# Group B's chunk outputs read in three steps on three engines

## The chip, the cores and the metric

The kernel runs on one core of one Trainium2 chip. The metric is the time of one execution on the device in microseconds (us); what is given is the median of several executions. The engines of the core each work through a queue of their own in order, and wait for each other by semaphores: TensorE (PE in the rows, with its weight loads as PEld), VectorE (DVE), ScalarE (ACT), GpSimd (POOL) and SyncE (SP), which issues most of the transfers.

## What is computed

One layer of a network over 2048 latent and 256 context tokens of width 1024: a modulated norm, one wide input projection, two groups of eight heads, and an output projection. Group B is the one that matters here: a gated delta rule in both directions, in chunks. Cut to its step, with `s` the 128 x 128 state of a head and a direction:

```
v_new = u0_i - einsum(w_i, s)
s_new = d_last * s + einsum(k_dec, v_new)
o     = einsum(q_dec, s) + einsum(p_i, v_new)
out   = o_forward + flip(o_backward)
```

The output `o` of a chunk is a sum of two products. One needs only the old state, the other needs the chunk's solved values `v_new`. The next chunk needs `s_new` alone.

## The kernel before

Tokens are taken in groups of 256 (two chunks of 128). A step of the program takes one token group of one head through the input projection and, in the same step, other heads' later stages: group A's unit, the keys, values and inverse of group B, and group B's chunks, forward for one head and backward for another. All of that is written as generators that are interleaved, and a scheduler with a clock of its own then orders the instructions of every engine. So a change of a few lines moves instructions all over the program.

Group B's chunk is `chain` (L873). It runs 272 times (16 context chunks without an output among them), so 256 chunks have an output: 128 of them come first in their token group and leave `o` in the tile `op` (`first` is true), and 128 come second, load what the first left (`o<-od`, L971) and add to it in the tile `o`. For every chunk there is one PSUM tile `pc`, a bank with four 128 x 128 places, one buffer for each direction:

- L889 writes `p1`, the keys times the state, and L891 writes `o1`, the queries times the state
- L893 (VectorE) makes `r` of `p1`; L894 multiplies it by the masked inverse `zb` into `p2`
- L897 and L900 (ScalarE) read `p2` twice, as `ud` for the state and as `u` for the output
- L902 writes `p3` from `ud`; L907 (VectorE) makes the new state `S` of it
- L911 writes the second part of the output into `p1`, from the masked scores `P` and `u`
- `out` (L973) reads both parts: for `first`, L975 (ScalarE) copies the second part to `op`, and L976 (VectorE) scales `o1` by the column `neb` and subtracts the copy. Otherwise L978 (VectorE) adds the scaled `o1` to `o`, and L979 (VectorE) subtracts the second part

The tile `pc` is guarded as a whole: an instruction that writes one of its places waits until those written ahead of it have read the others. In the built order 233 of the 256 instructions of L911 wait for the state update L907, which reads another place, and L902 waits for `u` in 236 of 272. The next chunk of the direction gets the same buffer, so its L889 waits for L976 or L979.

GpSimd masks `zb` and `P` (L920), multiplies in the SiLU (L769), scales keys of group A (L1219), and adds a bias to rows of decays (L788). All that it works on here lies in SBUF.

Of the kernel before, what the change touches and what calls it, by code (L numbers as in the profile page):

```python
# [13 lines left out]
ALU = mybir.AluOpType  # L14
# [4 lines left out]
P = 128  # L19
# [601 lines left out]
class BHead:  # L621
# [251 lines left out]
    def chain(self, d, gi, c, out, last):  # L873


        K, nc, h = self.K, self.K.nc, self.h
        q = self.q[gi]
        s = self.S[d]
        i = gi * GC + c

        def col(t):
            return t[:, d, h, i:i + 1]
        zb = q[f"zb{d}"][:, c, :]
        pc = K.pc.tile([P, 4, P], F32, tag=f"c{d}", name="pc")
        p1, p2, p3, o1 = (pc[:, j, :] for j in range(4))
        if s is None:
            r = q["v"][:, c, :]
        else:
            nc.tensor.matmul(p1, lhsT=q["kT"][:, c, :], rhs=s, start=True, stop=True)  # L889
            if out is not None:  # L890
                nc.tensor.matmul(o1, lhsT=q["qT"][:, c * P:c * P + P], rhs=s, start=True, stop=True)  # L891
            r = K.ck.tile([P, P], F32, tag=f"r{d}", name="r")
            nc.vector.scalar_tensor_tensor(r, p1, col(K.neb), q["v"][:, c, :], op0=ALU.mult, op1=ALU.add)  # L893
        nc.tensor.matmul(p2, lhsT=zb, rhs=r, start=True, stop=True)  # L894
        if not last:
            ud = K.ck.tile([P, P], F32, tag=f"ud{d}", name="ud")
            nc.scalar.activation(ud, p2, AF.Copy, scale=q["rk"][:, 1 + d, c:c + 1])  # L897
        if out is not None:
            u = K.ck.tile([P, P], F32, tag=f"u{d}", name="u")
            nc.scalar.activation(u, p2, AF.Copy, scale=q["rk"][:, 0, c:c + 1])  # L900
        if not last:
            nc.tensor.matmul(p3, lhsT=q["kn"][:, c, :], rhs=ud, start=True, stop=True)  # L902
            sn = K.ck.tile([P, P], F32, tag=f"S{d}", name="S", bufs=2 + d)
            if s is None:
                nc.vector.tensor_copy(sn, p3)
            else:
                nc.vector.scalar_tensor_tensor(sn, s, col(K.el), p3, op0=ALU.mult, op1=ALU.add)  # L907
            self.S[d] = sn
        if out is not None:

            nc.tensor.matmul(p1, lhsT=q[f"P{d}"][:, c, :], rhs=u, start=True, stop=True)  # L911
            out(c, o1, col(K.neb), p1)

    def masked(self, gi, d):

# [36 lines left out]
    def group(self, gi, d, first):  # L952


        K, nc = self.K, self.K.nc
        q = self.q[gi]
        if not first and d == 1:
            self.load_kk(gi, "kb", BB)
            q["vq"] = K.rt.tile([P, 3, GT], F32, tag="vqb", name="vq", bufs=BB)
            nc.sync.dma_start(q["vq"], q.pop("vq_d"))  # L960
            self.vqp(gi)
            q["ZZ"] = K.rt.tile([P, GC, P], F32, tag="ZZb", name="ZZ", bufs=BB)
            nc.sync.dma_start(q["ZZ"], q.pop("ZZ_d"))
        self.masked(gi, d)
        if first:
            o = K.gt.tile([P, GC, P], F32, tag="op", name="op")
        else:
            g = K.ho.tile([P, GC, P], F32, tag="gl", name="gl")
            nc.sync.dma_start(g, q["gate"])
            o = K.ho.tile([P, GC, P], F32, tag="ol", name="o")  # L970
            nc.sync.dma_start(o, q["o"])  # L971

        def out(c, o1, neb, o2):  # L973
            if first:
                nc.scalar.copy(o[:, c, :], o2)  # L975
                nc.vector.scalar_tensor_tensor(o[:, c, :], o1, neb, o[:, c, :], op0=ALU.mult, op1=ALU.subtract)  # L976
            else:
                nc.vector.scalar_tensor_tensor(o[:, c, :], o1, neb, o[:, c, :], op0=ALU.mult, op1=ALU.add)  # L978
                nc.vector.tensor_tensor(o[:, c, :], o[:, c, :], o2, op=ALU.subtract)  # L979
        for j in range(GC):  # L980
            c = GC - 1 - j if d else j
            self.chain(d, gi, c, out, j == GC - 1 and gi == (1 if d else NG))
            if j < GC - 1:
                yield
        if first:
            od = q["o"] = K.drg.tile([P, GC, P], F32, tag="od", name="od")
            nc.sync.dma_start(od, o)
        else:
            head_out(K, o, g, q["rq"], gi, 1024 + P * self.h)
        yield  # L990
# [152 lines left out]
def head_out(K, o, g, rq, gi, col):  # L1143


    nc = K.nc
    n = o.shape[1]
    ss = K.sm.tile([P, n], F32, tag="oss", name="oss")
    jk = K.gt.tile([P, P], F32, tag="jk", name="jk")
    for c in range(n):  # L1150
        nc.scalar.activation(jk, o[:, c, :], AF.Square, accum_out=ss[:, c:c + 1])
    r = K.sm.tile([P, n], F32, tag="or", name="or")
    if rq is None:
        nc.gpsimd.tensor_scalar(ss, ss, 1.0 / (P * P), EPS, op0=ALU.mult, op1=ALU.add)
        pow_rsqrt(K, r, ss)
        nc.gpsimd.tensor_scalar(r, r, P ** -0.5, None, op0=ALU.mult)
    else:
        nc.gpsimd.tensor_mul(ss, ss, rq[:, 1, :])
        nc.gpsimd.tensor_scalar(ss, ss, EPS, None, op0=ALU.add)
        pow_rsqrt(K, r, ss)  # L1160
        nc.gpsimd.tensor_mul(r, r, rq[:, 0, :])
    for c in range(n):
        nc.vector.scalar_tensor_tensor(o[:, c, :], o[:, c, :], r[:, c:c + 1], g[:, c, :], op0=ALU.mult, op1=ALU.mult)
    t0 = (gi - 1) * n * P
    nc.scalar.dma_start(K.y_d[t0:t0 + n * P, col:col + P].rearrange("(c p) n -> p c n", p=P), o)
# [522 lines left out]
```

## Time and profile before

| | us |
|---|---|
| median of 3 runs | 3420.04 |
| lowest and highest | 3418.63, 3421.8 |
| the profiled execution | 3429.3 |
| its span, first to last instruction | 3427.6 |
| busy: PE, DVE, ACT, POOL | 3135.9, 2459.6, 1839.5, 1473.7 |

The profile is of one execution. An engine's busy time beside the span tells how near it is to being the bound; what ended its idle time tells whom it waited for. TensorE's busy time is modelled for pipelined matmuls, so it is not work at full speed. The granted clock is the share of TensorE's full clock that it was given.

### The profile page before, as it was taken

How to read it: one execution, taken by the hardware profiler on the slowest of the kernel's cores; microseconds unless marked ns; L12 is line 12 of the kernel's file. 1: busy time of each engine (PE TensorE's matmuls, PEld its weight loads, DVE VectorE, ACT ScalarE, POOL GpSimd, SP SyncE). 2: the span in 40 equal slices, each digit the busy share in tenths (PEclk: the TensorE clock that was granted, in tenths of full speed). 3: DMA queues.
4: the chain of work that ended last, by engine and by line, in shares of the span. 5: the costliest groups of instructions: out<-in, count | busy, mean ns of one | idle time of the engine just before them, and what ended most of it. 6: DMA issues, size and time to landing. Idle time of an engine off the chain costs nothing.

```text
span 3427.6 us, 95270 instructions
## 1 busy us (share of the span) xinstructions
PE 3135.9 (91%) x37768; PEld 2428.1 (71%) x37768; DVE 2459.6 (72%) x6531; ACT 1839.5 (54%) x4921; POOL 1473.7 (43%) x2534
## 2 busy tenths in 40 slices
PE   7878998999998999899999999999999899898998
PEld 3666777877787777777777777777777677755554
DVE  5867687778877876788678867886788677845332
ACT  5764555555655564556565555556455654644332
POOL 3525644465446443644464446444444243521010
PEclk9999999999999999999999999999999999999999
DMA  7744444454445444555455444544354544544331
GB/s 248 233 146 140 133 128 145 138 173 145 148 143 166 149 141 124 164 152 153 130 168 151 149 136 154 155 126 143 126 155 137 188 149 139 158 148 149 136 117 51
DMA packets 433475, 508.45 MB, mean 148 GB/s; under 512 B 110724, under 2 KB 336644, under 8 KB 420996
## 3 DMA queue, kind: packets, MB, share of 16 engines
q1 hardware_dynamic: 395908, 477.18, 44.4%
q10 hardware_dynamic: 37120, 25.18, 2.3%
q8 instruction: 297, 4.87, 0.6%
q14 instruction: 150, 1.23, 0.1%
HBM read 346.35 MB, written 155.88 MB: 147 GB/s over the span
## 4 chain that ended last, share of the span: by engine, by line
PE 39%; DVE 21%; DMA 16%; POOL 9%; ACT 8%; issue 5%; SPq 1%; ACTq 0%; DVEq 0%; POOLq 0%
PE po L1535 8%; DVE acc L690 5%; PE pm L405 4%; PE pm L407 4%; PE pm L406 4%; DMA raw<-in_w_in_dram 3%; DMA df<-dd 3%; DVE QK L1279 2%; POOL br L788 2%; POOL or L56 2%; DMA dc<-dc_d 2%; PE pz L398 2%; PE pz L396 2%; PE pz L397 1%; DMA y_d<-df 1%
## 5 line engine op out<-in xcount | busy, mean ns | idle before, releaser
L405 PE MATMUL pm<-h,whi 128*128 128x256 f16 x3256 | 900.3, 276 | 13.8 <-ACT pad L652 5.6
L407 PE MATMUL pm<-h,wlo 128*128 128x256 f16 x3256 | 898.9, 276 | 2.6 <-DVE wlo L388 2.6
L406 PE MATMUL pm<-h,whi 128*128 128x256 f16 x3256 | 899.3, 276 | 0.0
L690 DVE SCALAR_TENSOR_TENSOR acc<-pad,cw,acc 128x504 f32<-128x504 f32 (+1 forms) x768 | 585.6, 766 | 26.8 <-ACT acc L684 17.4
L396 PE MATMUL pz<-whi,h 128*128 128x384 f16 (+1 forms) x1152 | 362.0, 318 | 19.8 <-ACT pad L652 6.3
L406 PEld LDWEIGHTS <-whi 128*128 128x128 f16 x3328 | 330.9, 99 | 56.4 <-issue 14.4
L407 PEld LDWEIGHTS <-wlo 128*128 128x128 f16 x3328 | 330.7, 99 | 46.4 <-DVE wlo L388 3.9
L405 PEld LDWEIGHTS <-whi 128*128 128x128 f16 x3328 | 331.2, 100 | 44.9 <-ACT whi L385 2.0
L398 PE MATMUL pz<-whi,h 128*128 128x384 f16 (+1 forms) x1152 | 361.8, 318 | 0.0
L397 PE MATMUL pz<-wlo,h 128*128 128x384 f16 (+1 forms) x1152 | 361.4, 318 | 0.0
L1267 ACT COPY sk<-QK 128x512 f32<-128x512 f32 x384 | 242.4, 631 | 203.0 <-DVE QK L1279 150.6
L1279 DVE TENSOR_TENSOR QK<-QK,T 128x512 f32<-128x512 f32 x384 | 267.8, 697 | 49.0 <-ACT sk L1267 39.1
L1219 POOL TENSOR_SCALAR QK<-QK,omlb 128x256 f32<-128x256 f32 x144 | 154.9, 1083 | 210.4 <-ACT QK L1215 209.3
L788 POOL TENSOR_SCALAR br<-br,nbc 128x128 f32<-128x128 f32 x252 | 175.4, 712 | 81.5 <-DMA br<-row_d 55.3
L897 ACT ACTIVATE ud<-pc,rk 128x128 f32<-128x128 f32 x272 | 99.7, 367 | 171.8 <-PE pc L894 146.4
L920 POOL TENSOR_SCALAR_AFFINE_SELECT zb<-zb 128x256 f32<-128x256 f32 x144 | 68.4, 476 | 271.3 <-ACT zb L925 258.6
L1535 PEld LDWEIGHTS <-yh 128*128 128x128 f16 x1024 | 100.3, 98 | 110.2 <-ACT yh L1523 1.5
L542 POOL TENSOR_TENSOR g<-w,lm 128x128 f32<-128x128 f32 (+2 forms) x120 | 81.3, 677 | 208.6 <-DVE w L591 91.8
L397 PEld LDWEIGHTS <-h 128*128 128x128 f16 x1152 | 114.8, 100 | 78.6 <-issue 25.6
L398 PEld LDWEIGHTS <-h 128*128 128x128 f16 x1152 | 114.5, 99 | 61.5 <-issue 3.2
L396 PEld LDWEIGHTS <-h 128*128 128x128 f16 x1152 | 114.7, 100 | 56.7 <-issue 3.0
L920 POOL TENSOR_SCALAR_AFFINE_SELECT P<-vq 128x256 f32<-128x256 f32 x128 | 70.0, 548 | 181.1 <-PE pc L911 126.4
(368 smaller groups left out, 8074.9 us busy)
## 6 DMA issues: line engine op xcount, KB each, us to landing
h<-hT SPq DMA_DIRECT2D x72, 1024.0 KB
raw<-in_w_in_dram SPq DMA_DIRECT2D x72, 512.0 KB
kk<-kk_d SPq DMA_DIRECT2D x137, 256.0 KB
df<-dd SPq DMA_DIRECT2D x64, 512.0 KB
vq_d<-vq SPq DMA_DIRECT2D x56, 384.0 KB
vq<-vq_d SPq DMA_DIRECT2D x56, 384.0 KB
kk_d<-kk SPq DMA_DIRECT2D x72, 256.0 KB
br<-row_d SPq DMA_DIRECT2D x48, 384.0 KB
```

The costliest lines, as they stand in the source:

```text
L396: nc.tensor.matmul(out, lhsT=h(0, k), rhs=w[0][:, k, :], start=(k == 0), stop=False)
L397: nc.tensor.matmul(out, lhsT=h(0, k), rhs=w[1][:, k, :], start=False, stop=False)
L398: nc.tensor.matmul(out, lhsT=h(1, k), rhs=w[0][:, k, :], start=False, stop=(k == KC - 1))
L405: nc.tensor.matmul(out, lhsT=w[0][:, k, :], rhs=h(0, k), start=(k == 0), stop=False)
L406: nc.tensor.matmul(out, lhsT=w[0][:, k, :], rhs=h(1, k), start=False, stop=False)
L407: nc.tensor.matmul(out, lhsT=w[1][:, k, :], rhs=h(0, k), start=False, stop=(k == KC - 1))
L690: nc.vector.scalar_tensor_tensor(av[:, :, a:b], pad[:, 1 + dy:R + 1 + dy, a + dx:b + dx], wt(dy, dx), av[:, :, a:b], op0=ALU.mult, op1=ALU ...
L788: (nc.vector if h < 1 else nc.gpsimd).tensor_scalar(t[:, c, :], t[:, c, :], K.nbc[:, d, h, b + c:b + c + 1], None, op0=ALU.add)
L1219: nc.gpsimd.tensor_scalar(QK[:, 3 - 2 * d, :], QK[:, 3 - 2 * d, :], col(K.omlb, d), None, op0=ALU.mult)
L1267: nc.scalar.copy(view(sk, m, [[-m, 2], [2 * m, 2 * np_], [1, m]]), view(QK, m, [[2 * n - m, 2], [2 * m, 2 * np_], [1, m]]))
L1279: nc.vector.tensor_tensor(qk, qk, view(T, 0, [[nT + 1, 2], [2, 2 * np_], [0, m]]), op=ALU.mult)
L1535: nc.tensor.matmul(po[b], lhsT=l[:, j, :], rhs=r[k][:, b * 512:(b + 1) * 512], start=f, stop=e)
```

## The change

`out` is called twice. The first call stands right behind `r`: VectorE reads `o1` and writes it, scaled by `neb`, to `op` (a plain scale, L983 of the changed kernel) or adds it to `o` (L985). The product of `P` and `u` moves ahead of the state update (L907 of the changed kernel, right behind L904, which writes `p3`). Behind the state update (L913), ScalarE copies `p1` into the tile of `u` (L917), and GpSimd subtracts that from `op` or `o` in SBUF (L981). VectorE's L976 and L979 are gone.

```diff
             nc.vector.scalar_tensor_tensor(r, p1, col(K.neb), q["v"][:, c, :], op0=ALU.mult, op1=ALU.add)
+            if out is not None:
+                out(c, o1, col(K.neb))
...
             nc.tensor.matmul(p3, lhsT=q["kn"][:, c, :], rhs=ud, start=True, stop=True)
+        if out is not None:
+
+            nc.tensor.matmul(p1, lhsT=q[f"P{d}"][:, c, :], rhs=u, start=True, stop=True)
+        if not last:
             sn = K.ck.tile([P, P], F32, tag=f"S{d}", name="S", bufs=2 + d)
...
-            nc.tensor.matmul(p1, lhsT=q[f"P{d}"][:, c, :], rhs=u, start=True, stop=True)
-            out(c, o1, col(K.neb), p1)
+            nc.scalar.copy(u, p1)
+            out(c, u, None)
...
-        def out(c, o1, neb, o2):
-            if first:
-                nc.scalar.copy(o[:, c, :], o2)
-                nc.vector.scalar_tensor_tensor(o[:, c, :], o1, neb, o[:, c, :], op0=ALU.mult, op1=ALU.subtract)
+        def out(c, x, neb):
+            if neb is None:
+                nc.gpsimd.tensor_tensor(o[:, c, :], o[:, c, :], x, op=ALU.subtract)
+            elif first:
+                nc.vector.tensor_scalar(o[:, c, :], x, neb, None, op0=ALU.mult)
             else:
-                nc.vector.scalar_tensor_tensor(o[:, c, :], o1, neb, o[:, c, :], op0=ALU.mult, op1=ALU.add)
-                nc.vector.tensor_tensor(o[:, c, :], o[:, c, :], o2, op=ALU.subtract)
+                nc.vector.scalar_tensor_tensor(o[:, c, :], x, neb, o[:, c, :], op0=ALU.mult, op1=ALU.add)
```

The order that the scheduler made is shown at one chunk, the first of token group 4, forward, of the fourth head of group B (`pc_23876` before, `pc_23975` after; the numbers at the names tell buffers apart, and what stands in brackets is the engine whose semaphore the instruction waits for). TensorE before, from the chunk's `p3` to the next chunk's L889:

```order
L902 MATMUL pc_23876<-ud_23882,kk_22824 128x128 [waits Activation_49]
L405 LDWEIGHTS whi_17398
...
L1335 MATMUL po_23827<-S_23816,QK_23179 128x128 [waits DVE_49]
L911 MATMUL pc_23876<-u_23884,P_23873 128x128 [waits DVE_49]
L1395 MATMUL po_23894<-S_23176,df_23892 128x128 [waits DMAHW4_49,Activation_49]
...
L889 MATMUL pc_24052<-S_23887,kk_22824 128x128 [waits DVE_49]
L891 MATMUL pc_24052<-S_23887,vq_22903 128x128
```

And TensorE after:

```order
L904 MATMUL pc_23975<-ud_23982,kk_22918 128x128 [waits Activation_49]
L907 MATMUL pc_23975<-u_23984,P_23972 128x128 [waits Pool_49]
L407 LDWEIGHTS wlo_17463
...
L889 MATMUL pc_24153<-S_23988,kk_22918 128x128
L891 MATMUL pc_24153<-S_23988,vq_22997 128x128
```

The output product now stands next to `p3`, with no other work between, and no longer waits for VectorE; here it waits for GpSimd, which masks `P`. VectorE, before, from `r` to the output of the chunk:

```order
L893 SCALAR_TENSOR_TENSOR r_23879<-pc_23876,neb_2218,vq_22903 128x128 [waits PE_49]
L1140 SCALAR_TENSOR_TENSOR g_23483<-pz_23772,wv_19235,g_23483 128x2x128 [waits Activation_49]
...
L907 SCALAR_TENSOR_TENSOR S_23887<-S_23329,el_2219,pc_23876 128x128 [waits PE_49]
...
L976 SCALAR_TENSOR_TENSOR op_23875<-pc_23876,neb_2218,op_23875 128x128 [waits Activation_49]
```

And after:

```order
L893 SCALAR_TENSOR_TENSOR r_23978<-pc_23975,neb_2218,vq_22997 128x128 [waits PE_49]
L983 TENSOR_SCALAR op_23974<-pc_23975,neb_2218 128x128
L690 SCALAR_TENSOR_TENSOR acc_24426<-pad_22898,cw_344,acc_24426 128x512 [waits DVE_49]
...
L913 SCALAR_TENSOR_TENSOR S_23988<-S_23428,el_2219,pc_23975 128x128 [waits PE_49]
```

The scale of `o1` has moved up from the chunk's end to right behind `r`, ahead of the convolution (L690). GpSimd after, around the subtraction, which has no counterpart before (`o_23949` is the other direction's chunk, `QK` belongs to group A):

```order
L745 TENSOR_TENSOR rk_23725<-de_2220,rk_23725 128x4 [waits Pool_49]
L981 TENSOR_TENSOR o_23949<-o_23949,u_23960 128x128 [waits DMAHW7_49,DMAHW2_49,Activation_49]
L981 TENSOR_TENSOR op_23974<-op_23974,u_23984 128x128 [waits DMAHW4_49,Activation_49]
L1225 TENSOR_SCALAR QK_24002<-QK_24002,omlb_2172 128x256 [waits DMAHW4_49,Activation_49]
L1225 TENSOR_SCALAR QK_24002<-QK_24002,omlb_2172 128x256
```

Two subtractions wait there for ScalarE's copies, and group A's scaling of `QK` stands behind them.

## Rows read from the trace of the kernel before

**Rows 1.** The page's first lines: span, busy time (share) x instructions.

```profile
span 3427.6 us, 95270 instructions
PE 3135.9 (91%) x37768; PEld 2428.1 (71%) x37768; DVE 2459.6 (72%) x6531; ACT 1839.5 (54%) x4921; POOL 1473.7 (43%) x2534
```

**Rows 2.** Two stretches: busy PE, PEld, DVE, ACT, POOL, then granted clock, DMA.

```profile
800.00:900.00 100.00, 94.40 (x1223) 79.29 (x1224) 84.46 (x234) 56.95 (x159) 43.11 (x68) 1.00 0.48 142
2700.00:2800.00 100.00, 88.39 (x1231) 70.77 (x1230) 69.68 (x175) 58.77 (x155) 44.50 (x62) 0.93 0.52 170
```

**Rows 3.** TensorE's waits, whole span: total us, times, longest us.

```profile
PE pc L894 <- DVE r L893: 22.3, 24, 2.6
PE pt L703 <- POOL vt L769: 13.1, 10, 2.0
...
PE pc L902 <- ACT u L900: 12.1, 8, 3.0
...
PE pc L911 <- DVE S L907: 9.8, 13, 2.0
PE pc L894 <- POOL zb L920: 9.4, 8, 1.9
...
PE pk L834 <- POOL vq L769: 4.7, 5, 1.2
...
PE pc L889 <- DVE o L979: 4.6, 6, 1.1
...
PE pc L889 <- DVE op L976: 3.7, 5, 1.0
```

**Rows 4.** TensorE in order of time, one late chunk: start, us, idle before.

```profile
3095.63 0.49 PE L889 MATMUL pc<-S,kk 128*128 128x128 f32 x2 [0.77 <-DVE o L979]
3095.95 0.39 PE L891 MATMUL pc<-S,vq 128*128 128x128 f32 x2
3098.98 0.80 PE L894 MATMUL pc<-r,zb 128*128 128x128 f32 x2 [2.64 <-DVE r L893]
3101.35 0.79 PE L902 MATMUL pc<-ud,kk 128*128 128x128 f32 x2 [1.57 <-ACT u L900]
3104.14 0.79 PE L911 MATMUL pc<-u,P 128*128 128x128 f32 x2 [2.00 <-DVE S L907]
```

**Rows 5.** Groups by shape, VectorE and ScalarE: busy us, mean ns, idle before.

```profile
L907 DVE SCALAR_TENSOR_TENSOR S<-S,el,pc 128x128 f32<-128x128 f32 x256 | 87.0, 341 | 72.2 <-PE pc L902 71.3
L978 DVE SCALAR_TENSOR_TENSOR o<-pc,neb,o 128x128 f32<-128x128 f32 x128 | 44.0, 344 | 37.4 <-PE pc L911 29.1 <-DMA o<-od 7.9
L976 DVE SCALAR_TENSOR_TENSOR op<-pc,neb,op 128x128 f32<-128x128 f32 x128 | 43.6, 343 | 18.9 <-ACT op L975 18.6
L979 DVE TENSOR_TENSOR o<-o,pc 128x128 f32<-128x128 f32 x128 | 35.7, 279 | 1.3
L975 ACT COPY op<-pc 128x128 f32<-128x128 f32 x128 | 34.0, 266 | 46.0 <-PE pc L911 32.0 <-DVE S L1385 6.9 <-DVE S L907 6.4
```

**Rows 6.** VectorE's copy of a PSUM place, line L905: ns least, median, most.

```profile
L905 DVE COPY S<-pc x16: 274/284/292, 351.5 to 2832.5; 128x128 f32<-128x128 f32 x16
```

**Rows 7.** GpSimd's group of two-input operations on 128 x 128, by shape.

```profile
L542 POOL TENSOR_TENSOR g<-w,lm 128x128 f32<-128x128 f32 x72 | 45.6, 633 | 107.0 <-DVE w L566 39.0 <-PE lv L610 31.2 <-DVE ww L504 19.8
```

**Rows 8.** VectorE, groups by shape: the state of group A from PSUM and from SBUF, and two large groups with SBUF operands.

```profile
L690 DVE SCALAR_TENSOR_TENSOR acc<-pad,cw,acc 128x504 f32<-128x504 f32 x576 | 440.7, 767 | 20.3 <-ACT acc L684 17.4
L1279 DVE TENSOR_TENSOR QK<-QK,T 128x512 f32<-128x512 f32 x384 | 267.8, 697 | 49.0 <-ACT sk L1267 39.1 <-PE sa L1369 8.4
...
L1385 DVE SCALAR_TENSOR_TENSOR S<-S,T,df 128x128 f32<-128x128 f32 x120 | 47.7, 398 | 83.7 <-DMA df<-dd 78.5 <-PE po L1395 4.5
L1385 DVE SCALAR_TENSOR_TENSOR S<-S,T,kv 128x128 f32<-128x128 f32 x136 | 46.3, 340 | 5.5 <-PE kv L1311 4.1
```

**Rows 9.** A piece of the chain that ended last: start us, us, what.

```profile
3306.40 19.42 PE po L1535 x90
```

**Rows 10.** The mean granted clock of the core.

```profile
core 0: 3427.6 us, clock 0.972
```

## The prediction

> **What bounds the kernel now.** The engines' busy times come first: TensorE is busy for 3135.9 us of a span of 3427.6, VectorE for 72%, ScalarE for 54%, GpSimd for 43% [rows 1]. TensorE sets the end, and what a change can give back is a part of its 291.7 idle us (3427.6 less 3135.9), or of what its clock costs. The two stretches show both: between 800 and 900 us TensorE is busy for 94.40 of 100 at a granted clock of 1.00; between 2700 and 2800 for 88.39 at 0.93 [rows 2]. Over the core the mean is 0.972 [rows 10], so about 96 us (0.028 x 3427.6) go to stretches at the lower level, 1.2 instead of 2.4 GHz, which is 0.33 us for each idle us. I use that ratio as an estimate of what an idle us brings along.
>
> Then TensorE's waits by who ended them [rows 3]. They are short and many, and group B's tile `pc` has the longest: for `r` before L894 22.3 us in 24 waits, for `u` before L902 12.1 in 8, for the state before L911 9.8 in 13, for the masked `zb` 9.4 in 8, for the end of the output before the next L889 4.6 + 3.7 in 11. That is 61.9 us, a fifth of the idle time. Where the scheduler has other work to put between, the chunk costs nothing; where it hasn't, every stop shows. In one such chunk at 3095 us TensorE stood 0.77 us for the output, 2.64 for `r`, 1.57 for `u` and 2.00 for the state [rows 4].
>
> **What the change does to these stops, one by one.** All terms are TensorE's idle time.
>
> *The stop for the state goes.* The output product waited for L907, which only shares its PSUM tile. It now stands behind `p3`, whose wait for `u` is the one it needs itself. The row gives 9.8 us [rows 3], and nothing takes its place at that stop unless the mask `P` is late, which was needed there before too. The state now waits for one more product, 0.4 us of matmul or so by the 0.39 to 0.79 us of such pairs [rows 4]; it is needed at the next L889 only. Term: -9.8.
>
> *The stop for the output at the next L889.* Before, the output product was followed by 266 + 343 ns (copy and VectorE) or by 344 + 279 ns (VectorE twice) [rows 5], and then the tile was free. Now it is followed by the state update, 341 ns, and ScalarE's copy, 266 ns [rows 5]: in the built order the copy waits for the state in 240 of 256 chunks. So 607 ns against 609 and 623, the same. But the room has grown: counted in the built orders, the matmul columns (a float32 one as four) between the output product and the next L889 of its direction go from 10,600 to 13,800 in the median and from 7,200 to 7,900 in the shortest tenth. 90 matmuls of 512 columns took 19.42 us [rows 9], 0.42 ns a column, so that is 4.5 to 5.8 us in the median. I take half of the 8.3 us of this stop as gone, with 0 and 8.3 as bounds. Term: -4.
>
> *The stop for r.* L894 now waits for the scale of `o1` as well, which stands behind `r` on VectorE: 344 ns where it adds to `o`, and where it only scales, about the 284 ns of a copy of the same PSUM shape [rows 5, 6]. In 24 waits that is 24 x 0.31 = 7.5 us if nothing else moves. The columns between L891 and this matmul grew from 7,800 to 9,500 in the median and from 5,100 to 5,900 in the shortest tenth, 0.70 and 0.32 us: just what the added step takes. I take 0, with +7.5 and -8 as bounds. The add to `o` also needs its transfer `o<-od` a good half of a chunk earlier; VectorE waits for it now for 7.9 us [rows 5], and a doubling of that, if it all reached TensorE, lies in the upper bound.
>
> *The stop for u.* ScalarE's two reads of `p2` are the same, and so is their room (7,900 columns before, 7,400 after in the median, 5,500 to 6,000 in the shortest tenth). New is a wait on GpSimd: the copy reuses the tile of `u`, so the next chunk's `u` must wait for the subtraction, in 147 of 256 chunks by the order. Behind it on ScalarE stand other evictions. It has some 13,800 + 9,500 columns or nearly 10 us to be done in, against a subtraction of less than 1 us. Term 0 there, up to +5.
>
> *VectorE is relieved.* 128 x 279 ns (L979) and 128 x (343 - 284) ns go: 35.7 + 7.6 = 43.3 us [rows 5, 6], 1.8% of its busy time. Against it stand the collisions with GpSimd. The same state update of group A takes 340 ns with one operand in PSUM and 398 with both in SBUF [rows 8], so 58 ns are paid for SBUF operands with GpSimd at 43%. GpSimd gets 4.7% of the span more (below), so 6 ns more for each of some 2,000 such instructions, L690 and L1279 with 960 of them among these [rows 8]: 12 us. What is left, 31 us or 1.3%, makes VectorE a little less late for the idle time that isn't `pc`'s (291.7 - 61.9 = 230 us, most of which other rows share out): at that share -3, of which I take -2, with 0 and -4 as bounds.
>
> The Trainium skill (SBUF — State Buffer, on the shared port pair) has it that an operation of VectorE with two SBUF inputs and a GpSimd operation that reads SBUF lock each other out for a whole instruction. The rise from 340 to 398 ns agrees that something is paid, though far from a whole instruction in the mean [rows 8]. Taken at its word, an added chance of 4.7% to meet half of a 633 ns operation would cost 15 ns an instruction, 30 us as an estimate, and VectorE would still be relieved by 13; the sum would lose 1 us. So that page speaks against a part of the gain on VectorE and doesn't turn it.
>
> *ScalarE gets the other 128 copies*, 128 x 266 ns = 34 us [rows 5], 1.9% of its work. Term: +1.
>
> *GpSimd gets 256 subtractions.* The trace of before has none on these tiles; the nearest is a two-input operation of the same shape at 633 ns in the mean [rows 7], and nothing is cheaper than VectorE's 279 [rows 5]. At 633 it is 162 us, 11% more GpSimd. TensorE stood 13.1 + 9.4 + 4.7 = 27.2 us for GpSimd in the three rows that matter [rows 3]; 11% of that is +3. Each subtraction also waits at the head of GpSimd's queue for a copy, and masks, SiLU products and group A's scaling stand behind it. I take +5 for both, with 0 and a doubling (+27) as bounds.
>
> **Sum.** -9.8 - 4 + 0 + 0 - 2 + 1 + 5 = -9.8 us idle, and with 0.33 us of clock for each, -13. From the profiled execution's 3429.3 us that gives 3416; the runs have a median of 3420.04, 9.3 below the profiled one, and the same step from there gives 3407.
>
> **Rivals.** (1) *GpSimd's queue becomes the late one* (slower). If the stops before subtractions hold up the masks and SiLU products so that TensorE's 27.2 us for GpSimd double, the term is +27 instead of +5, the sum +12, with the clock +16: 3436. It decides from a rise of 15 us in these rows, over half. For it: the subtraction waits for a copy that waits for the state that waits for a product, and TensorE stands 13.1 us for a SiLU product and 9.4 us for a mask as it is [rows 3]. Against it: GpSimd is idle for 57%, and nothing that TensorE needs at once comes from a subtraction. 20%.
> (2) *The gain is passed on* (no change). The state's stop goes, but `p3` and the output product now hang on one stop, `u`, whose room has not grown; the scheduler has drawn every engine's order anew, and some 230 idle us that have nothing to do with `pc` fall out differently. With the 9.8 us returned at `u` and elsewhere: 3420. 25%.
> (3) *All of pc's stops shrink*, since the chunk has one stop less and more work between the others: -9.8 - 8.3 - 8 - 4 = -30, with the clock -40: 3380. For it: the room grew at two stops; against it: the longest row, `r`, has a longer step now. 13%.
> The forecast itself gets 42%.
>
> A measurement of this kernel tells about 0.2% or 7 us from no change. The forecast lies 13 below, so a small part of it falls within 7; with (3) faster has 0.52, same 0.27, slower 0.21. The range, from part of the way to (3) to most of (1): 3385 to 3433.
>
> **What would show it.** In the changed kernel's waits on TensorE no row of the output product for the state; the row of L896 (the old L894) for VectorE near 22 us, now for the scale; the row of L889 for ScalarE's copy well under 8 us. VectorE's busy time near 2430 us, ScalarE's near 1873, GpSimd's near 1636 with a group of 256 subtractions at about 633 ns. Wrong would be: rows for GpSimd on TensorE together over 42 us (rival 1); `u`'s row over 20 us (rival 2); the scale's stop at 30 us or more with `o<-od` behind it. If TensorE's idle time outside `pc` and GpSimd's rows has moved by over 15 us, then the redrawn order decided, and none of the steps.

## The result, and the profile after

The changed kernel takes 3452.15 us in the median of 4 runs (3446.86 to 3463.64), against 3420.76 for the kernel before beside it: a ratio of 1.0097, with a 95% interval of 1.007 to 1.0124. It is slower by about 31 us. The forecast was 13 us faster, and the time lies beyond the range's upper end of 3433. The profiled execution took 3449.44 us, 20.1 more than the profiled one of before, so the two traces show some two thirds of the loss, and the columns below, of one execution each, no more than that.

The page's first lines and the mean clock, to hold against [rows 1] and [rows 10]:

```profile
span 3447.7 us, 95606 instructions
...
PE 3133.8 (91%) x37768; PEld 2419.2 (70%) x37768; DVE 2439.5 (71%) x6403; ACT 1861.5 (54%) x5049; POOL 1600.6 (46%) x2790
...
core 0: 3447.7 us, clock 0.969
```

The span is split into three for what follows, as the prediction did for before: *idle* (span less PE's busy time), *clock* (what the mean clock falls short of 1, times the span; two us either way by the rounding of the clock), and *rest*, the busy time less the clock's part, which stands for the matmuls at full clock with the gaps that the trace doesn't show as idle.

| us | span | idle | clock | rest | `pc`'s waits | all other waits |
|---|---|---|---|---|---|---|
| before | 3427.6 | 291.7 | 96.0 | 3039.9 | 70.6 | 206.6 |
| after | 3447.7 | 313.9 | 106.9 | 3026.9 | 42.5 | 250.6 |

The last two columns are sums over the rows of TensorE's waits. So the change lost 22 us of idle and 11 of clock, and won 13 us in the rest, which the prediction had no term for. VectorE has 20 us less work, ScalarE 22 more, GpSimd 127 more, each at two thirds to four fifths of the forecast's 31, 34 and 162. The groups of the new steps on ScalarE, GpSimd and VectorE, with busy us, mean ns and the idle time before them, beside [rows 5]:

```profile
L917 ACT COPY u<-pc 128x128 f32<-128x128 f32 x256 | 67.0, 265 | 139.6 <-DVE S L913 132.1 <-PE pc L907 5.6 <-DVE T L1294 1.1
...
L981 POOL TENSOR_TENSOR o<-o,u 128x128 f32<-128x128 f32 x128 | 73.5, 575 | 230.1 <-ACT u L917 220.1 <-DMA dd<-QK 9.3
...
L981 POOL TENSOR_TENSOR op<-op,u 128x128 f32<-128x128 f32 x128 | 71.4, 559 | 95.6 <-ACT u L917 94.4
...
L985 DVE SCALAR_TENSOR_TENSOR o<-pc,neb,o 128x128 f32<-128x128 f32 x128 | 43.5, 340 | 22.4 <-DMA o<-od 22.4
L983 DVE TENSOR_SCALAR op<-pc,neb 128x128 f32<-128x128 f32 x128 | 43.3, 338 | 0.0
```

Two new waits are large: ScalarE stands 132.1 us at the head of its queue for the state update, and GpSimd over 300 us for the copies. TensorE's own waits (total us, times, longest), beside [rows 3]:

```profile
PE pt L703 <- POOL vt L769: 24.1, 16, 2.6
PE po L1341 <- DVE S L1391: 21.9, 13, 3.2
PE po L1401 <- DVE vq L835: 12.5, 5, 3.0
...
PE pc L896 <- DVE op L983: 11.1, 16, 1.5
...
PE pt L1311 <- DVE QK L1285: 9.2, 10, 1.6
PE sa L1372 <- DVE QK L1285: 8.9, 12, 2.0
...
PE pc L904 <- ACT u L902: 7.2, 11, 2.0
...
PE pc L889 <- ACT u L917: 4.7, 6, 1.4
...
PE pc L896 <- DVE o L985: 3.8, 4, 2.3
...
PE pc L896 <- POOL zb L926: 3.0, 3, 1.2
```

On the tile `pc` the change does more than was hoped: all of the chunk's rows together fall by 28 us. Everything else rises by 44. The longest rows now belong to work that the change never touches: the transposes of the values (L703), group A's state and output (L1341, L1401), its other products (L1311, L1372). By who ended the waits, VectorE's went from 138 to 165 us, GpSimd's only from 37 to 42, ScalarE's fell from 72 to 62.

Such a row names the last link alone. One stop at L703, followed back through the timelines of TensorE, GpSimd, ScalarE and VectorE (start us, us, what, the idle time before it):

```profile
1186.82 0.44 PE L703 MATMUL pt<-ident,vt 128*128 128x128 f32 x2 [2.38 <-POOL vt L769]
...
1185.86 0.91 POOL L769 TENSOR_TENSOR vt<-acc,sg 128x256 f32<-128x256 f32 x1 [2.73 <-ACT sg L768]
...
1185.36 0.72 ACT L768 ACTIVATE sg<-acc 128x256 f32<-128x256 f32 x2 [3.57 <-DVE acc L690]
...
1184.32 0.35 DVE L1391 SCALAR_TENSOR_TENSOR S<-S,T,df 128x128 f32<-128x128 f32 x1 [1.29 <-DMA df<-dd]
1184.59 1.40 DVE L690 SCALAR_TENSOR_TENSOR acc<-pad,cw,acc 128x504 f32<-128x504 f32 x2
```

TensorE waits for GpSimd, GpSimd for ScalarE's sigmoid, that for VectorE's convolution, and the convolution stood behind a state update that waited for a transfer. No subtraction stands in this chain. This one stop shows lateness running through the in-order queues, but not which part of the change made them late. That takes experiments.

### The profile page after: what moved, and what is told of

It reads as the page before. It is cut to its first block, busy times and chain, and to the rows that moved or that the text cites. A ratio compares the mean times of both kernels' runs of the same rounds, so it can differ in the third digit from the quotient of the medians.

```text
span 3447.7 us, 95606 instructions
## 1 busy us (share of the span) xinstructions
PE 3133.8 (91%) x37768; PEld 2419.2 (70%) x37768; DVE 2439.5 (71%) x6403; ACT 1861.5 (54%) x5049; POOL 1600.6 (46%) x2790
## 5 line engine op out<-in xcount | busy, mean ns | idle before, releaser
L690 DVE SCALAR_TENSOR_TENSOR acc<-pad,cw,acc 128x504 f32<-128x504 f32 (+1 forms) x768 | 585.4, 767 | 20.9 <-ACT acc L684 11.8
L396 PE MATMUL pz<-whi,h 128*128 128x384 f16 (+1 forms) x1152 | 358.0, 316 | 18.2 <-DVE g L1146 10.9
L398 PE MATMUL pz<-whi,h 128*128 128x384 f16 (+1 forms) x1152 | 358.1, 316 | 0.0
L981 POOL TENSOR_TENSOR o<-o,u 128x128 f32<-128x128 f32 x128 | 73.5, 575 | 230.1 <-ACT u L917 220.1
L397 PEld LDWEIGHTS <-h 128*128 128x128 f16 x1152 | 113.4, 98 | 79.0 <-issue 22.7
L398 PEld LDWEIGHTS <-h 128*128 128x128 f16 x1152 | 113.2, 98 | 62.1 <-issue 1.2
L768 ACT ACTIVATE sg<-acc 128x256 f32<-128x256 f32 x208 | 79.7, 414 | 142.5 <-DVE acc L690 115.1
```

Of the source, the lines that this page charges most:

```text
L396: nc.tensor.matmul(out, lhsT=h(0, k), rhs=w[0][:, k, :], start=(k == 0), stop=False)
L397: nc.tensor.matmul(out, lhsT=h(0, k), rhs=w[1][:, k, :], start=False, stop=False)
L398: nc.tensor.matmul(out, lhsT=h(1, k), rhs=w[0][:, k, :], start=False, stop=(k == KC - 1))
L690: nc.vector.scalar_tensor_tensor(av[:, :, a:b], pad[:, 1 + dy:R + 1 + dy, a + dx:b + dx], wt(dy, dx), av[:, :, a:b], op0=ALU.mult, op1=ALU ...
```

## The experiments

All ratios are to the kernel before, run on the same chip beside them, with a 95% interval (the medians of before differ by up to 14 us from chip to chip). The main theories, tried in turn, are these: (O) the order that the scheduler drew anew is unlucky; (A) ScalarE's copy waits for the state update at the head of its queue and everything behind it is late; (D, E) the added work on GpSimd (D) or ScalarE (E) costs more than the few microseconds it was priced at. The recorded expectations name narrower ones too, B, C, F and G, and say there what each means. A kernel with an added instruction in it has an order of its own, so one result differs from another by a draw of the order as well.

### Is it the draw of the order?

One unneeded fill on VectorE at the start (1024 columns in a, 256 in b) was put into both kernels:

```diff
-    K.mone = cp.tile([P, 4], F32, name="mone")
+    K.mone = cp.tile([P, 4], F32, name="mone"); nc.vector.memset(cp.tile([P, 1024], F32, name="idle"), 0.0)
```

> The kernel before with one idle fill of a 128 x 1024 tile on VectorE (about 1 us) at the start, which nothing reads. It makes the scheduler draw another order for a third of TensorE's rows. If the result of the change was a draw of the order (theory: redrawn order), this kernel too moves by some 0.5 to 1% either way, to 3400 or 3440 us and more. If the change's own steps decide (theories: ScalarE's waiting copy, or GpSimd), it stays within 0.3% of 3420 us, plus the 1 us of the fill.

> The kernel before with a smaller idle fill (128 x 256) on VectorE at the start: another draw of the order, with a fifth of TensorE's rows moved. Redrawn order: a time of its own, 0.5% or more from the other draws. Own steps: within 0.3% of 3420 us.

> The changed kernel with the same idle fill at the start. Redrawn order: it comes out anywhere between 0.99 and 1.015 of the kernel before. The change's own steps: it stays at 1.007 to 1.012, and ScalarE again stands over 100 us for the state update ahead of its copy.

> The changed kernel with the smaller idle fill. Redrawn order: a time of its own, 0.5% or more from the other draws of the changed kernel. Own steps: again 1.007 to 1.012 of the kernel before.

| kernel | median us | ratio | interval |
|---|---|---|---|
| before, redrawn a | 3427.79 | 0.9991 | 0.9972 to 1.001 |
| before, redrawn b | 3418.68 | 0.9965 | 0.9951 to 0.9979 |
| after, redrawn a | 3467.53 | 1.011 | 1.0082 to 1.0139 |
| after, redrawn b | 3461.14 | 1.0083 | 1.0053 to 1.0112 |

A draw is worth up to 0.35%; three draws of the changed kernel lie at 1.0083 to 1.011, three of before at 0.9965 to 1. The loss comes back in every draw, so (O) falls, as far as such fills redraw the order (a third and a fifth of TensorE's rows, by the expectations). The same rows stand at the head of TensorE's waits in all three draws of after (L703 24.1, 24.5 and 25.3 us; L1341 21.9, 22.4 and 21.1).

### The parts one by one

The product alone is moved ahead of the state update, the output read as before (L975 to L979 unchanged):

```diff
+        if out is not None:
+            nc.tensor.matmul(p1, lhsT=q[f"P{d}"][:, c, :], rhs=u, start=True, stop=True)
         if not last:
             sn = K.ck.tile([P, P], F32, tag=f"S{d}", name="S", bufs=2 + d)
...
-            nc.tensor.matmul(p1, lhsT=q[f"P{d}"][:, c, :], rhs=u, start=True, stop=True)
             out(c, o1, col(K.neb), p1)
```

> The kernel before with one part of the change: the product of P and u stands ahead of the state update; the output is read as before, behind it. Theory A (ScalarE stands at its copy for the state update, and what is queued behind it is late): half of the chunks, the first ones, already have a copy on ScalarE that would now wait for the state too, so 0.3 to 0.5% slower. Theory B (the state comes later, since it waits for one more product): 1.005 or more with every reader unchanged. Theory C (VectorE's early scale, with the wait for o<-od at the head of its queue): no change or 0.997, as the stop of 9.8 us goes.

It takes 3413.35 us, 0.9939 (0.9917 to 0.9961): a gain of 0.6%, which none of the three theories in its expectation had, though ScalarE's copy of the second part waits for the state update here too (its group on ScalarE):

```profile
L977 ACT COPY op<-pc 128x128 f32<-128x128 f32 x128 | 33.5, 261 | 81.1 <-DVE S L910 78.7 <-DVE T L1290 2.0
```

The scale alone is moved up behind `r`; the product stays behind the state, and VectorE subtracts it from PSUM:

```diff
+            if out is not None:
+                out(c, o1, col(K.neb))
...
-            out(c, o1, col(K.neb), p1)
+            out(c, p1, None)
...
+                nc.vector.tensor_tensor(o[:, c, :], o[:, c, :], x, op=ALU.subtract)
```

> The kernel before with another part alone: VectorE scales o1 right behind r, the product of P stands where it stood, and VectorE subtracts it straight from PSUM; no copy, no GpSimd. Theory C: this is where the loss is, 1.007 to 1.01, with VectorE standing some 20 us for o<-od. Theories A and B: no loss, 0.995 to 1.001, as ScalarE is rid of 34 us of copies.

3443.02 us, 1.0027 (1.0007 to 1.0047): by itself it gains nothing, and theory C, which put 0.7 to 1% of loss here, is too large. VectorE's wait for the transfer `o<-od` is 20.7 us here, as in the changed kernel (22.4), against 7.9 before [rows 5].

Both moves together, VectorE subtracting from PSUM: the change without ScalarE's copies and GpSimd's subtractions.

```diff
-            nc.scalar.copy(u, p1)
-            out(c, u, None)
+            out(c, p1, None)
...
-                nc.gpsimd.tensor_tensor(o[:, c, :], o[:, c, :], x, op=ALU.subtract)
+                nc.vector.tensor_tensor(o[:, c, :], o[:, c, :], x, op=ALU.subtract)
```

> The changed kernel, but at the end VectorE subtracts the product straight from PSUM: early scale and the product ahead of the state, no copy on ScalarE, nothing on GpSimd. Theory A and the theory that GpSimd's subtractions cost it: 0.994 to 1.000, the whole loss is gone. Theories B and C: the loss stays, 1.006 or more.

3404.26 us, 0.992 (0.989 to 0.9949). **This version beats both kernels.** Its page, three of TensorE's waits, the group of the moved product on TensorE and VectorE's later subtraction (busy us, mean ns, idle before):

```profile
PE 3119.0 (92%) x37768; PEld 2423.9 (71%) x37768; DVE 2472.0 (73%) x6659; ACT 1810.5 (53%) x4793; POOL 1484.9 (44%) x2534
...
PE po L1340 <- DVE S L1390: 25.5, 20, 3.5
...
PE pc L896 <- DVE o L984: 7.6, 9, 2.1
...
PE pc L889 <- DVE op L980: 2.2, 5, 0.6
...
L907 PE MATMUL pc<-u,P 128*128 128x128 f32 x512 | 101.9, 281 | 0.8 <-POOL P L925 0.8
...
L980 DVE TENSOR_TENSOR o<-o,pc 128x128 f32<-128x128 f32 x128 | 35.8, 280 | 9.2 <-PE pc L907 9.1
```

The same product in the kernel before:

```profile
L911 PE MATMUL pc<-u,P 128*128 128x128 f32 x512 | 107.5, 293 | 9.9 <-DVE S L907 9.8
```

The stop at group A's state (L1340, L1341 of the changed kernel) is as long here, so it is no sign of the copies. Then ScalarE's copy put back, with VectorE subtracting it in SBUF instead of GpSimd:

```diff
-                nc.gpsimd.tensor_tensor(o[:, c, :], o[:, c, :], x, op=ALU.subtract)
+                nc.vector.tensor_tensor(o[:, c, :], o[:, c, :], x, op=ALU.subtract)
```

> The changed kernel with the copy on ScalarE, but the subtraction of it on VectorE instead of GpSimd. Theory A: the loss stays, 1.006 to 1.012, and ScalarE again stands over 100 us for the state update. Theory D (GpSimd's 256 subtractions, their 137 us and the stops in its queue are the loss): 0.998 to 1.003.

3455.52 us, 1.0063 (1.0041 to 1.0085). The copy in the chunk's path turns a gain of 0.8% into a loss of 0.6%, with no work added to GpSimd. ScalarE's group of copies, the longest of TensorE's waits and VectorE's subtractions:

```profile
L917 ACT COPY u<-pc 128x128 f32<-128x128 f32 x256 | 67.1, 264 | 134.1 <-DVE S L913 127.5 <-PE pc L907 3.8 <-DVE T L1294 1.4
...
PE pc L896 <- DVE o L985: 30.4, 29, 4.0
...
L981 DVE TENSOR_TENSOR o<-o,u 128x128 f32<-128x128 f32 x128 | 39.8, 311 | 16.4 <-ACT u L917 15.6
L981 DVE TENSOR_TENSOR op<-op,u 128x128 f32<-128x128 f32 x128 | 39.3, 307 | 8.9 <-ACT u L917 8.8
```

VectorE now stands 24.4 us for the copies at the head of its queue, where it stood 9.1 for the product, and TensorE's stop for VectorE at L896 (`o` alone) goes from 7.6 to 30.4.

Both results were drawn once more with the 1024-column fill, since they carry the verdict:

> The kernel of both_vector_reads (0.992) with an idle fill of a 128 x 1024 tile on VectorE at the start, for another draw of the order. If its gain is the moved product's and not a draw's: 0.989 to 0.996. If a draw's: 0.996 or more.

> The kernel of copy_vector_subtracts (1.0063: copy on ScalarE, subtraction on VectorE) with the same idle fill. If GpSimd has a part of the loss: again 1.003 to 1.008, under the four draws of the change with GpSimd (1.0083 to 1.0111). If GpSimd has none: 1.008 to 1.011.

3400.24 us, 0.9919 (0.9899 to 0.994), and 3456.58 us, 1.0081 (1.0059 to 1.0102). Both hold. But 1.0081 lies at the border of what its expectation called "GpSimd has none" of the loss, level with the lowest draw of the changed kernel, 1.0083. The split for these kernels, with the same columns; each is of the profiled execution, which can stand apart from the median (early scale 18 us under it, the redrawn copy 11 over it):

| us | span | idle | clock | rest | `pc`'s waits | all other waits |
|---|---|---|---|---|---|---|
| before, redrawn a | 3425.6 | 286.5 | 95.9 | 3043.2 | 68.0 | 201.8 |
| before, redrawn b | 3425.0 | 297.1 | 92.5 | 3035.4 | 73.4 | 208.9 |
| early scale only | 3423.6 | 280.4 | 106.1 | 3037.1 | 76.7 | 189.8 |
| product ahead only | 3411.6 | 295.5 | 95.5 | 3020.6 | 46.9 | 234.5 |
| both moves | 3404.9 | 285.9 | 105.6 | 3013.4 | 34.0 | 237.1 |
| both moves, redrawn | 3402.9 | 296.0 | 91.9 | 3015.0 | 40.0 | 239.5 |
| and the copy | 3453.1 | 320.1 | 114.0 | 3019.0 | 61.2 | 241.5 |
| and the copy, redrawn | 3464.8 | 322.8 | 131.7 | 3010.3 | 74.2 | 235.4 |
| after, redrawn a | 3464.7 | 329.2 | 110.9 | 3024.6 | 39.5 | 270.8 |
| after, redrawn b | 3449.4 | 320.7 | 103.5 | 3025.2 | 42.0 | 260.1 |

Three things are to be read here. The rest is 3035 to 3043 where the product stands behind the state and 3010 to 3027 wherever it has moved: in these executions that is the whole gain. (The column charges all of the lower clock to busy time. Counted in the traces, only the part that falls on busy time taken off, every rest is 13 to 22 us higher and the two groups stay apart: 3053 to 3056 against 3028 to 3043.) The idle time isn't less in the versions that gain: what `pc`'s stops lose, other stops take (28 to 64 us more than before, in the kernels of this table with the product moved). And the copy costs idle time at `pc` again where VectorE subtracts (61 and 74, at the scale of `o1` before L896 with `o<-od` in front), and at other places where GpSimd does (251 to 271).

### What is it in the copy?

Theory (A) says that it is the 132 us wait for the state. On top of the version with both moves, a ScalarE copy that nobody reads: first of `u`, which is there long before, then of the new state, which makes it wait as in the changed kernel.

```diff
+            w = K.ck.tile([P, P], F32, tag=f"w{d}", name="w")
+            nc.scalar.copy(w, u)                      # idle_copy
+            nc.scalar.copy(w, u if last else sn)      # state_copy
             out(c, p1, None)
```

> The kernel of both_vector_reads (0.992) with one more copy of u, 128 x 128 in SBUF, on ScalarE for each of the 256 chunks, into a tile that nothing reads: ScalarE's added work as in the change, without a wait and without PSUM. Theory A (the wait ahead of the copy costs it): 0.990 to 0.997. Theory E (ScalarE's added 70 us of work, wherever they stand): 1.003 or more.

> The kernel of both_vector_reads (0.992) with a copy on ScalarE of the new state, 128 x 128 in SBUF, for each chunk, into a tile that nothing reads: it waits for the state update as the change's copy does, but holds no PSUM tile, and nothing waits for it. Theory A: ScalarE stands some 130 us for the state and the time is 1.002 to 1.008. Theory F (the PSUM tile pc is held longer, or the output is late): as idle_copy, 0.990 to 0.997.

The copy that waits for nothing: 3426.7 us, 0.9989 (0.9975 to 1.0004). The one that waits for the state: 3431.66 us, 1.0004 (0.999 to 1.0017). Its group in the trace:

```profile
L918 ACT COPY w<-S 128x128 f32<-128x128 f32 x240 | 71.0, 296 | 125.9 <-DVE S L913 120.0 <-DMA y_d<-o 4.0 <-DVE o L982 0.6
```

ScalarE stands 120.0 us for the state there, and that adds 0.15%, within what the two intervals allow for nothing. So (A) falls: the long row on ScalarE is nearly free. (The product-ahead kernel said so already: 128 copies of the output wait 78.7 us for the state there, and it gains.) The copies that wait for nothing cost 0.7% on this kernel: in the profiled execution, beside the first draw of both moves, 11 us of idle time (296.6) and 14 of clock (120.0), with the rest as it was (3012.6); beside the redrawn one it is all clock. Both results lie between the ranges that their expectations gave to the theories, and neither kernel was drawn a second time.

Two more kernels touch the copy of the changed kernel itself. One puts it ahead of the state update, so that the state waits for the copy; the other gives it a tile of its own, so that `u` is free at once.

```diff
+            nc.scalar.copy(u, p1)     # copy_first: ahead of the state update
...
-            nc.scalar.copy(u, p1)
...
+            w = K.ck.tile([P, P], F32, tag=f"w{d}", name="w")     # own_tile
+            nc.scalar.copy(w, p1)
+            out(c, w, None)
```

> The changed kernel with ScalarE's copy written ahead of the state update: now the copy waits for TensorE alone and VectorE's state update waits for the copy. Theory A in its narrow form (a wait on ScalarE's queue for VectorE): 0.995 to 1.003, ScalarE's wait for the state is gone. Theory F: the state, and the chain with it, comes 266 ns later, 1.010 or more.

> The changed kernel with the copy in a tile of its own, so that the next chunk's u doesn't wait for GpSimd's subtraction. If that guard were the loss (theory G): 0.997 to 1.004. Theory A: 1.007 to 1.012 as the change itself.

3453.24 us, 1.0065 (1.0039 to 1.009), and 3469.52 us, 1.0111 (1.0083 to 1.0139). The first takes back 0.2 to 0.45% of the three draws of the changed kernel, no more than a draw is worth, and its interval overlaps the changed kernel's; the second takes back nothing, so the shared tile of `u` is no cause. In the first, ScalarE waits for the product instead:

```profile
L908 ACT COPY u<-pc 128x128 f32<-128x128 f32 x256 | 66.5, 267 | 98.4 <-PE pc L907 79.2 <-DVE df L1169 17.4 <-PE pt L1528 0.5
```

Last, a copy that reads the product itself, behind VectorE's subtraction, and that nobody reads: it keeps the PSUM tile in use, as the changed kernel's does, but the output doesn't wait for it.

```diff
             out(c, p1, None)
+            w = K.ck.tile([P, P], F32, tag=f"w{d}", name="w")
+            nc.scalar.copy(w, p1)
```

> The kernel of both_vector_reads (0.992) with a copy of the product from PSUM on ScalarE behind VectorE's subtraction, into a tile that nothing reads. ScalarE's work and its wait are the change's, and the PSUM tile is held until the copy is done, but neither VectorE nor GpSimd waits for its result. If holding the tile is the other half of the loss: 1.005 to 1.010, with TensorE's wait before L889 for the copy over 12 us. If not: as state_copy, 0.998 to 1.002.

3440.98 us, 1.0034 (1.0016 to 1.0053). That is 0.3 to 0.45% over the two copies that leave the PSUM tile alone; the rest, up to 1.0063 and 1.0081 with the output waiting for the copy, is another 0.3 to 0.5%. Each of these two steps is about as large as a draw of the order (0.35%), so they aren't shown one by one; what is shown, in two draws, is the whole of 1.4 to 1.6%. And the sign that was to go with a tile held too long, over 12 us before L889 for the copy, did not come: that row is 3.9 us.

### What is it in GpSimd?

GpSimd subtractions, 256 of them, of constants in SBUF and unread, on the version with both moves and on the kernel before; and, beside the latter, the idle copies of `u` on the kernel before.

The comments name the runs:

```diff
+            w = K.ck.tile([P, P], F32, tag=f"w{d}", name="w")
+            nc.gpsimd.tensor_tensor(w, K.ident, K.ones, op=ALU.subtract)   # idle_gpsimd, before_idle_gpsimd
+            nc.scalar.copy(w, u)                                          # before_idle_copy
```

> The kernel of both_vector_reads (0.992) with one subtraction of two constant 128 x 128 tiles in SBUF on GpSimd for each of the 256 chunks, into a tile that nothing reads. If GpSimd's work itself costs (its queue, and the SBUF collisions with VectorE): 0.996 to 1.000. If only stops in its queue or nothing: 0.990 to 0.995.

> The kernel before with one subtraction of two constant tiles on GpSimd for each of the 256 chunks, into a tile that nothing reads. If GpSimd's added work has a price of its own: 1.006 to 1.012. If it only spoiled the order of both_vector_reads: 0.998 to 1.003.

> The kernel before with one more copy of u, 128 x 128 in SBUF, on ScalarE for each of the 256 chunks, into a tile that nothing reads. If ScalarE's added work has a price of its own: 1.005 to 1.009. If it only spoiled the order of both_vector_reads: 0.998 to 1.003.

| kernel | median us | ratio | interval |
|---|---|---|---|
| both moves, idle subtractions | 3432.54 | 1.0014 | 0.9994 to 1.0034 |
| before, idle subtractions | 3489.5 | 1.0155 | 1.0121 to 1.019 |
| before, idle copies | 3424.51 | 0.9979 | 0.9962 to 0.9997 |

The copies cost the kernel before nothing, though they cost 0.7% on the other: that price isn't a general one, and the expectation's other reading, that they only spoiled the order of the version with both moves, isn't ruled out.

The subtractions seem to cost 0.95% (1.0014 against 0.992) and 1.55%, some 32 and 53 us, more than either expectation had. But they don't stand where the change's stand. They wait for nothing, and the scheduler put all 256 at the start of the kernel. The groups of both kernels (before and both moves with idle subtractions) with their first and last start, and of the changed kernel's subtractions:

```profile
L913 POOL TENSOR_TENSOR w<-ident,ones x256: 444/453/1870, 228.9 to 524.4; 128x128 f32<-128x128 f32 x128
...
L918 POOL TENSOR_TENSOR w<-ident,ones x256: 444/453/2608, 231.8 to 523.9; 128x128 f32<-128x128 f32 x128
...
L981 POOL TENSOR_TENSOR op<-op,u x128: 446/457/1602, 367.1 to 3067.7; 128x128 f32<-128x128 f32 x128
L981 POOL TENSOR_TENSOR o<-o,u x128: 448/458/1656, 613.1 to 3284.0; 128x128 f32<-128x128 f32 x128
```

So these runs price a burst, and the loss arises in it. In that stretch the kernel before gets through 3458 matmuls, with the idle subtractions through 3057 (busy PE, PEld, DVE, ACT, POOL, then granted clock, DMA; before, then with the subtractions):

```profile
225.00:525.00 300.00, 260.33 (x3458) 208.21 (x3455) 221.75 (x590) 159.73 (x372) 154.26 (x227) 0.95 0.45 138
...
225.00:525.00 300.00, 240.48 (x3057) 186.86 (x3054) 222.21 (x491) 136.60 (x311) 268.69 (x461) 0.92 0.38 115
```

At the first row's rate the 401 matmuls are about 35 us, an estimate; with both moves it is 524 (3448 to 2924), some 46 us, of which later stretches take some back (these two traces end 20 us apart). What the burst does to VectorE can be seen too. No instruction was added to it, and it is busy for 2494.3 us instead of 2459.6 [rows 1]; with both moves it is 2500.0 instead of 2472.0. That is 35 and 28 us, while fills and idle copies move it by about 3 at most. The page of the kernel before with idle subtractions, and the worst single case on VectorE, GpSimd and TensorE (start us, us, what, idle before):

```profile
PE 3158.0 (90%) x37768; PEld 2437.4 (70%) x37768; DVE 2494.3 (71%) x6531; ACT 1843.3 (53%) x4921; POOL 1596.6 (46%) x2790
...
368.45 7.58 DVE L541 TENSOR_TENSOR g<-w,lm 128x128 f32<-128x128 f32 x1
...
368.43 1.27 POOL L913 TENSOR_TENSOR w<-ident,ones 128x128 f32<-128x128 f32 x3
369.67 0.45 POOL L542 TENSOR_TENSOR g<-w,lm 128x128 f32<-128x128 f32 x1
370.08 5.80 POOL L913 TENSOR_TENSOR w<-ident,ones 128x128 f32<-128x128 f32 x14
...
376.08 0.24 PE L575 MATMUL lv<-g,mt 32*32 32x32 f32 x2 [2.43 <-DVE g L541]
```

A VectorE instruction with two inputs in SBUF took 7.58 us while 18 GpSimd instructions ran one behind the other, and TensorE stood 2.43 us for it. Its group, 72 of them, goes from a mean of 299 ns to 423, and this one makes up most of the rise:

```profile
L541 DVE TENSOR_TENSOR g<-w,lm 128x128 f32<-128x128 f32 x72 | 21.5, 299 | 13.0 <-PE lv L610 10.5 <-DMA w<-img 1.4 <-POOL P L920 0.5
...
L541 DVE TENSOR_TENSOR g<-w,lm 128x128 f32<-128x128 f32 x72 | 30.4, 423 | 16.8 <-PE lv L610 10.0 <-DMA w<-img 5.2 <-POOL w L913 1.4
```

In the changed kernel, whose subtractions are spread over the whole time, the same group is at 315 ns. What GpSimd costs there is told only by the kernel that differs in it alone: against VectorE subtracting the same copies, 1.0083 to 1.0111 stand over 1.0063 and 1.0081, 0 to 0.5%, 1 to 16 us, with VectorE rid of 79 us of subtractions. That is no more than draws of the order differ by. So the loss is shown to come with ScalarE's copy, once the output is read from it; that GpSimd's subtractions have a part in it (D) is not shown.

## Why the prediction was wrong, point by point

- **The stops on `pc`: right, and too low.** The state's stop is gone (the product waits 0.3 us for its mask, 9.8 before). The next L889 fell from 8.3 to 4.7, `r`'s stop from 22.3 to 14.9, `u`'s from 12.1 to 7.2, `zb`'s from 9.4 to 3.0. It was the third rival that described them: all shrink.
- **That `pc`'s stops are the gain: a failed step.** The steps -9.8 and -4 were taken as idle time won, with a share of clock on top. In every kernel with the product moved, other stops took it back; with both moves the idle time is 285.9 and 296.0 us, as in three draws of before (286.5 to 297.1). The gain of 0.6 and 0.8% is in the rest: some 20 us with the product ahead, 25 with both moves. A part of it stands in the product's own group, 107.5 to 101.9 us, 293 to 281 ns for one. Counted in the traces (each matmul up to the start of the next, the lower clock's time halved), the product's share of TensorE's busy time goes from 71 or 72 us to 62 or 63, and that of `p3` in front of it from 73 or 74 to between 67 and 71: 11 to 16 us together. Where the others are wasn't found.
- **The transfer `o<-od`: past its bound on VectorE, harmless there.** VectorE's wait rose from 7.9 to 22.4 us, nearly three times where a doubling was reckoned with; the stop before L896 for `o` is 3.8.
- **VectorE's relief: smaller.** The plain scale took 338 ns, not 284, which is 7 of the 43 us; collisions took 16 instead of 12 in the sum (2459.6 less 36.5 for the output's own groups is 2423, and 2439.5 was measured). The Trainium skill (SBUF — State Buffer, the section "SBUF: two separate sides") has it that a VectorE operation with two SBUF inputs and a GpSimd operation that reads SBUF lock each other out for a whole instruction. The trace of the burst agrees that VectorE stands still for GpSimd, but there through 18 instructions; and the 16 us of the changed kernel are nearer to the prediction's 12 than to the 30 that it estimated by that rule.
- **ScalarE's copies, +1: the term that failed.** It priced the added busy time, 1.9%, and nothing for the output's new way through ScalarE. With VectorE subtracting, putting the copies in costs 1.4 to 1.6% of the time, 49 to 55 us, in two draws: nearly the whole loss. The +1 was for 128 copies more, and the version without has none; but the product-ahead kernel still has the old 128, in the path of the output too, and lies only 0.2% behind, so the price isn't so much for each copy. The wait for the state, the longest new row on ScalarE, is 0.15% at most. The rest of the price stays open: added work (0.7% in one draw of one kernel, nothing on the kernel before), the PSUM tile held longer, the output waiting for the copy.
- **GpSimd's subtractions, +5 (0 to +27): not shown wrong.** The three rows that were to mark the first rival went from 27.2 to 30.0 us (24.1, 3.0 and 2.9 at L834), far from 42, and GpSimd instead of VectorE costs 1 to 16 us at the end. The group took 559 and 575 ns in the mean, not 633.
- **The second rival, the gain passed on: half right.** The stops were passed on, to places outside `pc`, and by over the 15 us that the last sign named (207 to 251, with GpSimd's rows, which took 9 of it). But the conclusion tied to that sign, that the redrawn order decides, was wrong: some 30 us of it come with the moved product (234.5 to 239.5), and the whole recurs in each draw of the changed kernel.
- **The sum.** A gain of about 27 us (0.8%) was there, from a term that the sum didn't have, and about 60 of loss (1.0097 less 0.992) hid it: 49 to 55 with the copies, 1 to 16 with GpSimd's subtractions in VectorE's place. By which queue a copy of 0.27 us, 256 times, costs some 50 us stays open; so does why idle copies cost 0.7% on one kernel and nothing on another.

## What to carry to other kernels

An instruction put on an engine that is idle half of the time can be far from free when another queue then has to wait for it: don't price it by its busy time or by the waits that name its engine, but build the kernel that differs in it alone, in more than one draw of the order. An unread stand-in prices it only if it runs where the real one does, so look up its first and last start before believing its price. Moving a product out from behind a wait that came only from a shared PSUM tile was worth 0.6%, 0.8% with its partner read early, though the idle time it freed went elsewhere; reading its result by way of ScalarE lost it again. When a change has a gaining and a losing part, run each alone: the sum showed only the loss, and the best version lay in the change itself.

## What the hardware showed that was not expected

- Packed into 295 us, 256 GpSimd subtractions of 0.56 to 0.60 us in SBUF lengthened VectorE's unchanged work by 28 to 35 us, with no data passing between them. One VectorE instruction that takes 0.30 us in the mean took 7.58.
- The plain scale from PSUM (338 ns) is no cheaper on VectorE than scale and add (340), while a copy of the same shape took 284 [rows 6].
- TensorE's busy time at full clock fell by 13 to 30 us for the same 37768 matmuls when one of the chunk's products moved next to another, out from behind a wait; which of the two it was wasn't tested.
